# Attention in a decoder trunk: the values product with tokens on the partitions, and scores begun one tile ahead

## The chip, the core and the metric

The kernel runs on one core of a Trainium2 chip. The metric is the device time of one execution in microseconds (us). Runs are compared by their median; the profile is one more execution, read by the hardware profiler.

## What is computed

Two layers of a decoder trunk on 512 tokens of width 1024, float32. Each layer is a feed-forward block, a mixer and a second feed-forward block. The mixer projects the tokens and sends them through three branches: attention with forget gates (FoX), a linear recurrence (RG-LRU) and RWKV-7. The branches are weighted by gates, added and projected. The change is in the attention branch, which has 8 heads of 64:

```
log_f = log_sigmoid(f_logit + f_bias)
F = cumsum(log_f, axis=1)
s = einsum('bhqd,bhkd->bhqk', q, k) * dh**-0.5
s = s + (F[..., :, None] - F[..., None, :])
s = where(kpos <= qpos, s, -inf)
p = softmax(s, axis=-1)
o = einsum('bhqk,bhkd->bhqd', p, v)
```

## The kernel before

Weights are streamed from memory. Large products are made in three passes of float32r halves (`mm3`, lines 201 to 203: hi by hi, lo by hi, hi by lo), so they are nearly all of TensorE's instructions. A weight tile is split into its halves by ScalarE (line 194) and by VectorE or, in the mixer, GpSimd (line 196).

In the mixer, `mix_branches` runs three generators beside each other. FoX attention and then the LRU yield a cost at each step; by the sum of these costs the loop of lines 1140 to 1152 advances the RWKV branch (with raised priority), the gate products (`gates`), and the background work that makes the next modulation (`bg_step`, VectorE line 284). A scheduler then sets a fixed order for each engine from the instructions' order in the program, priorities and its own costs. Each engine works through its list strictly in order; semaphores join the lists.

Attention handles two heads at a time (`fox_pair`, line 1013), so there are four pairs in each layer, eight in all. For a pair it makes q, k and v (lines 1024 to 1040): queries and keys with the 64 channels of a head on the partitions, values with the tokens on the partitions (`vs`). Then come four tiles of 128 queries (line 1047). Tile i sees the n+128 keys up to its own end, n = 128 i, and for each of its two heads:

- GpSimd adds the causal mask to the forget row (`fm`, line 1052);
- TensorE makes the scores, 128 queries on the partitions, in two products (1054, 1055);
- VectorE adds the forget row and finds the maximum, first for the last 128 keys (1058), then for those in front (1062), and negates it (1066);
- ScalarE makes the exponential `e` and its sum (1068);
- VectorE takes the sum's reciprocal (1069) and multiplies `e` by it (1070).

Then, for each head, TensorE transposes the i+1 blocks of `e` (1077) so that keys lie on the partitions, and ScalarE or VectorE copies the result `et` (1080, 1082). The values product (1089) has 64 value columns of one head as its stationary side and 128 queries of `et` moving, and writes head 0 to partitions 0 to 63 and head 1 to 64 to 127 of `po`; ScalarE copies this to `aout` (1091), which has channels on the partitions. Scores, transposes and values products all take PSUM tiles with the tag "s", of which the mixer has three, used in turn (`self.ps("s")`, line 143). `e` has two buffers.

## Time and profile before

| | us |
|---|---|
| median of 3 runs | 3094.02 |
| lowest, highest | 3092.88, 3103.51 |
| the profiled execution | 3098.59 |
| its span | 3096.5 |
| TensorE busy in the span | 2931.2 (95%) |
| VectorE busy | 1880.0 (61%) |
| ScalarE busy | 1142.2 (37%) |
| GpSimd busy | 554.8 (18%) |

PE is TensorE's matmul row, PEld its weight loads, DVE is VectorE, ACT ScalarE, POOL GpSimd, SP the queue that issues most loads. Busy times are of the span. Times in the text are microseconds from the span's start. A matmul's recorded duration includes its way through the array, so neighbours overlap: what one costs is the distance from its start to the next start. A float32 matmul is recorded as two instructions, a transpose as one.

### The profile page before, as it was taken

Reading aid. Unit: us, or ns where it says so; the run is one execution under the profiler, and the core shown is the slowest. Engines: PE = TensorE matmul, PEld = TensorE weight load, DVE = VectorE, ACT = ScalarE, POOL = GpSimd, SP = SyncE. Lnnn points to the kernel's source line nnn. Section 1 sums busy time; section 2 is a strip of 40 time slices with the busy share of each in tenths; the row PEclk is TensorE's granted clock in tenths of the full one; section 3 lists DMA queues with packets and bytes.
Section 4 is the critical chain, followed back from the end, with each engine's and each line's share of the span. In section 5 each row is a group of like instructions: output and inputs, shape, how many; then the busy total and the mean of one; then the engine's idle time right before and its main releaser. Section 6 shows DMA issues by size and latency. Waiting matters only on the chain. (4 is left out here: it accounts for less than half of the span.)

```text
span 3096.5 us, 39351 instructions
## 1 busy us (share of the span) xinstructions
PE 2931.2 (95%) x15330; PEld 2338.4 (76%) x15330; DVE 1880.0 (61%) x3534; ACT 1142.2 (37%) x1699; POOL 554.8 (18%) x379
## 2 busy tenths in 40 slices
PE   7999998998989998999999999889989899999998
PEld 5888886676766788888888887767666677788887
DVE  6755567666785656565656546667676756654435
ACT  4322253332545635222342214433335554342212
POOL 0000142333232013000130002423333320230000
PEclk9999999999999999999999999999999999999999
DMA  8634333333342463434434424433333424632221
GB/s 280 224 109 146 115 117 101 88 87 102 94 113 67 139 203 118 139 122 143 129 117 136 133 92 145 127 99 93 88 90 93 107 73 143 204 116 96 89 68 62
DMA packets 389402, 372.17 MB, mean 120 GB/s; under 512 B 54964, under 2 KB 318544, under 8 KB 389216
## 3 DMA queue, kind: packets, MB, share of 16 engines
q1 hardware_dynamic: 377048, 350.14, 37.0%
q10 hardware_dynamic: 12168, 19.53, 1.7%
q8 instruction: 120, 1.97, 0.3%
q14 instruction: 66, 0.54, 0.1%
HBM read 347.54 MB, written 22.09 MB: 119 GB/s over the span
## 5 line engine op out<-in xcount | busy, mean ns | idle before, releaser
L194 ACT ACTIVATE hi<-raw 128x1024 fp32r<-128x1024 f32 (+1 forms) x460 | 469.2, 1028 | 1248.9 <-PE pg L202 501.3
L196 POOL TENSOR_TENSOR lo<-raw,hi 128x1024 fp32r<-128x1024 f32 x164 | 408.0, 2490 | 1692.1 <-ACT hi L194 1639.2
L201 PE MATMUL pg<-hhi,hi 128*128 128x512 f32 (+1 forms) x1744 | 680.4, 393 | 13.7 <-DVE ks L645 3.7
L202 PE MATMUL pg<-hlo,hi 128*128 128x512 f32 (+1 forms) x1744 | 673.5, 389 | 2.9 <-DVE nm L343 2.9
L203 PE MATMUL pg<-hhi,lo 128*128 128x512 f32 (+1 forms) x1744 | 674.8, 391 | 0.0
L196 DVE TENSOR_TENSOR lo<-raw,hi 128x1024 fp32r<-128x1024 f32 (+1 forms) x296 | 342.5, 1165 | 301.3 <-ACT hi L194 296.1
L201 PEld LDWEIGHTS pg<-hhi,hi 128*128 128x128 f32 x1744 | 330.9, 190 | 86.9 <-issue 10.5
L203 PEld LDWEIGHTS pg<-hhi,lo 128*128 128x128 f32 x1744 | 330.6, 190 | 66.5 <-issue 2.1
L202 PEld LDWEIGHTS pg<-hlo,hi 128*128 128x128 f32 x1744 | 331.2, 190 | 65.3 <-issue 4.7
L202 PE MATMUL pr<-hlo,hi 128*128 128x512 f32 (+1 forms) x816 | 300.4, 368 | 5.1 <-DVE nm L343 2.9
L201 PE MATMUL pr<-hhi,hi 128*128 128x512 f32 (+1 forms) x816 | 301.5, 370 | 2.2 <-ACT hhi L397 2.2
L203 PE MATMUL pr<-hhi,lo 128*128 128x512 f32 (+1 forms) x816 | 300.7, 369 | 0.0
L284 DVE SCALAR_TENSOR_TENSOR acc<-raw,cact,acc 128x512 f32<-128x512 f32 x224 | 187.7, 838 | 48.7 <-DMA raw<-in_ada_w_dram 44.3
L202 PEld LDWEIGHTS pr<-hlo,hi 128*128 128x128 f32 x816 | 155.0, 190 | 34.2 <-issue 7.4
L201 PEld LDWEIGHTS pr<-hhi,hi 128*128 128x128 f32 x816 | 155.1, 190 | 28.1 <-ACT hhi L397 2.6
L203 PEld LDWEIGHTS pr<-hhi,lo 128*128 128x128 f32 x816 | 155.2, 190 | 27.4
L352 POOL TENSOR_TENSOR rstd<-var,mhalf 128x1 f32<-128x1 f32 x48 | 30.2, 630 | 470.5 <-DVE var L351 461.9
L201 PE MATMUL ps<-hi,ahi 128*128 128x512 f32 x264 | 103.5, 392 | 0.0
L203 PE MATMUL ps<-hi,alo 128*128 128x512 f32 x264 | 103.3, 391 | 0.0
L202 PE MATMUL ps<-lo,ahi 128*128 128x512 f32 x264 | 103.1, 391 | 0.0
L480 DVE TENSOR_TENSOR su<-pg,su 128x512 f32<-128x512 f32 x42 | 28.9, 689 | 115.2 <-PE pg L203 115.1
L480 DVE TENSOR_TENSOR su<-pr,su 128x512 f32<-128x512 f32 x42 | 29.0, 690 | 110.0 <-PE pr L203 105.9
(443 smaller groups left out, 4956.9 us busy)
## 6 DMA issues: line engine op xcount, KB each, us to landing
raw<-in_ffn_up_dram SPq DMA_DIRECT2D x70, 1024.0 KB
raw<-in_w_in_dram SPq DMA_DIRECT2D x132, 512.0 KB
raw<-in_ada_w_dram SPq DMA_DIRECT2D x64, 1024.0 KB
raw<-in_ffn_down_dram SPq DMA_DIRECT2D x40, 1024.0 KB
raw<-in_ffn_up_dram SPq DMA_DIRECT2D x36, 512.0 KB
gspill<-gate ACTq DMA_DIRECT2D x48, 256.0 KB
gate<-gspill SPq DMA_DIRECT2D x48, 256.0 KB
ada<-in_ada_w_dram SPq DMA_DIRECT2D x16, 512.0 KB
```

Of the source, the lines that this page charges most:

```text
L194: self.nc.scalar.activation(hi, v, AF.Copy)
L196: eng.tensor_tensor(out=lo, in0=v, in1=hi.bitcast(F32), op=ALU.subtract)
L201: mm(out=ps, lhsT=lhi, rhs=rhi, start=start, stop=False, **kw)
L202: mm(out=ps, lhsT=lhi, rhs=rlo, start=False, stop=False, **kw)
L203: return mm(out=ps, lhsT=llo, rhs=rhi, start=False, stop=stop, **kw).ins
L284: nc.vector.scalar_tensor_tensor(out=acc, in0=r[:, i, :], scalar=c, in1=acc, op0=ALU.mult, op1=ALU.add)
L352: nc.gpsimd.tensor_tensor(out=r, in0=v, in1=self.mhalf, op=ALU.pow)
L480: nc.vector.tensor_tensor(out=su, in0=pss[1], in1=su, op=ALU.mult)
```

## The change

The division is moved behind the values product, the values product is turned round, and the tiles are staggered.

- `scores(i)` holds lines 1048 to 1068 of before. It leaves the exponentials undivided, puts the sums of both heads side by side in one tile `rs` and takes one reciprocal for the two.
- `values(i)` holds the transposes and the values product. `et` is now the stationary side (128 queries wide) and 64 columns of one head's values move; the result has queries on the partitions, head 0 in columns 0 to 63, head 1 in columns 64 to 127. VectorE multiplies it by the reciprocals while it takes it out of PSUM, into `ao`.
- The order in the program is scores 0, scores 1, values 0, scores 2, values 1, scores 3, values 2, values 3. `e` gets four buffers for this.
- After the last tile TensorE transposes the four tiles of `ao`, and ScalarE copies them to `aout` in one instruction of 512 columns where there were four of 128.

```diff
-        for i in range(NT):
+        ao = ap.tile([P, NT, P], F32, tag="ao", bufs=1, name=self.nm("ao"))
+        def scores(i, es, rs):
             n = i * P
-            es = []
             for hh, fb in enumerate(fbs):
...
-                e = ap.tile([P, S], F32, tag="e", bufs=2, name=self.nm("e"))
+                e = ap.tile([P, S], F32, tag="e", bufs=4, name=self.nm("e"))
...
-                rs = self.sp.tile([P, 1], F32, tag="rsum", name=self.nm("rsum"))
-                nc.scalar.activation(e[:, 0 : n + P], e[:, 0 : n + P], AF.Exp, bias=nm, accum_out=rs)
-                nc.vector.reciprocal(rs, rs)
-                nc.vector.tensor_scalar(out=e[:, 0 : n + P], in0=e[:, 0 : n + P], scalar1=rs, scalar2=None, op0=ALU.mult)
+                nc.scalar.activation(e[:, 0 : n + P], e[:, 0 : n + P], AF.Exp, bias=nm, accum_out=rs[:, hh : hh + 1])
                 es.append(e)
                 yield 0.2 * (i + 1)
+            nc.vector.reciprocal(rs, rs)
+
+        def values(i, es, rs):
+            n = i * P
             ets = []
...
             po = self.ps("s")
-            for j in range(i + 1):
-                for hh, et in enumerate(ets):
-                    mm(out=po[64 * hh : 64 * hh + 64, 0:P], lhsT=vs[:, j, hh * 64 : hh * 64 + 64],
-                       rhs=et[:, j * P : (j + 1) * P], start=j == 0, stop=j == i, skip_group_check=True)
-            nc.scalar.activation(self.aout[:, p, n : n + P], po[:, 0:P], AF.Copy)
+            for hh, et in enumerate(ets):
+                for j in range(i + 1):
+                    mm(out=po[:, 64 * hh : 64 * hh + 64], lhsT=et[:, j * P : (j + 1) * P],
+                       rhs=vs[:, j, hh * 64 : hh * 64 + 64], start=j == 0, stop=j == i, skip_group_check=True)
+            nc.vector.tensor_tensor(out=ao[:, i, :].rearrange("p (h d) -> p h d", h=2), in0=po[:, 0:P].rearrange("p (h d) -> p h d", h=2),
+                                    in1=rs.unsqueeze(2).to_broadcast([P, 2, DH]), op=ALU.mult)
             yield 0.25 * (i + 1)
+
+
+        tiles = [([], self.sp.tile([P, 2], F32, tag="rsum", name=self.nm("rsum"))) for _ in range(2)]
+        yield from scores(0, *tiles[0])
+        for i in range(NT):
+            if i + 1 < NT:
+                if i:
+                    tiles.append(([], self.sp.tile([P, 2], F32, tag="rsum", name=self.nm("rsum"))))
+                yield from scores(i + 1, *tiles[i + 1])
+            yield from values(i, *tiles[i])
+        pt = self.ps("s")
+        for i in range(NT):
+            nc.tensor.transpose(pt[:, i * P : (i + 1) * P], ao[:, i, :], self.ident)
+        nc.scalar.activation(self.aout[:, p, :], pt, AF.Copy)
```

In the changed kernel the transposes of `e` have line 1078, the copies of `et` 1081 and 1083, the reciprocal 1070, the values product 1090, the division 1092, and the transposes at the end 1107. The lists of the engines show where the scheduler puts this.

TensorE, the first pair of the first layer, from the scores of tile 0 (lines 1054 and 1055, 128 keys) on; `pg` are other branches' products, `ps` the three tiles in turn. Before:

```order
L1055 MATMUL ps_3940<-kl_3494,q_3575 128x128
L1054 MATMUL ps_3954<-k_3576,q_3575 128x128
L1055 MATMUL ps_3954<-kl_3494,q_3575 128x128
L201 MATMUL pg_4172<-hhi,hi_4173 128x512
...
L1077 MATMUL ps_3966<-ident,e_3943 128x128
...
L1077 MATMUL ps_3970<-ident,e_3957 128x128
L203 MATMUL pg_4172<-hhi,lo_4174 128x512
L1089 MATMUL ps_3974<-et_3968,v_3577 64x128
L1089 MATMUL ps_3974<-et_3972,v_3577 64x128
```

Twelve other products stand between the scores and the first transpose, five between the two transposes, one in front of the values product. Now:

```order
L1055 MATMUL ps_3943<-kl_3494,q_3575 128x128
L1055 MATMUL ps_3954<-kl_3494,q_3575 128x128
L1055 MATMUL ps_3966<-kl_3494,q_3575 128x256
L1055 MATMUL ps_3978<-kl_3494,q_3575 128x256
L201 MATMUL pg_4164<-hhi,hi_4165 128x512
L202 MATMUL pg_4164<-hlo,hi_4165 128x512
L1078 MATMUL ps_4009<-ident,e_3946 128x128
...
L1078 MATMUL ps_4013<-ident,e_3957 128x128
...
L1090 MATMUL ps_4017<-v_3577,et_4011 128x64
L1090 MATMUL ps_4017<-v_3577,et_4015 128x64
```

(Of each score the first product, line 1054, is left out here.) The scores of tile 1 (256 keys) have moved in front of tile 0's transposes, and two other products are left between scores and first transpose, with six between the transposes and six in front of the values product.

VectorE at the same place, from the second head's negated maximum of tile 0 to the copy of `et`; lines 866 and 868 are the RWKV branch, 284 the background work. Before:

```order
L1066 TENSOR_SCALAR nmx_3960<-mx_3958 128x1
L284 SCALAR_TENSOR_TENSOR acc_4204<-raw_4483,cact,acc_4204 128x512
L868 TENSOR_TENSOR Y_3705<-Y_3705,T_3704 64x6x10
L1069 RECIPROCAL rsum_3948<-rsum_3948 128x1
L284 SCALAR_TENSOR_TENSOR acc_4204<-raw_4483,cact,acc_4204 128x512
L866 TENSOR_TENSOR T_3704<-Y_3705 64x63
L1070 TENSOR_SCALAR e_3943<-e_3943,rsum_3948 128x128
...
L1070 TENSOR_SCALAR e_3957<-e_3957,rsum_3962 128x128
L868 TENSOR_TENSOR Y_3705<-Y_3705,T_3704 64x8x8
L1082 COPY et_3968<-ps_3966 128x128
```

Now:

```order
L1066 TENSOR_SCALAR nmx_3960<-mx_3958 128x1
L284 SCALAR_TENSOR_TENSOR acc_4196<-raw_4474,cact,acc_4196 128x512
L868 TENSOR_TENSOR Y_3705<-Y_3705,T_3704 64x6x10
L1058 ISA e_3969,mx_3970<-ps_3966,fm_3964 128x128
L866 TENSOR_TENSOR T_3704<-Y_3705 64x63
L1062 ISA e_3969,mx_3970<-ps_3966,fb_3933,mx_3970 128x128
...
L1070 RECIPROCAL rsum_3939<-rsum_3939 128x2
...
L1062 ISA e_3981,mx_3982<-ps_3978,fb_3935,mx_3982 128x128
L866 TENSOR_TENSOR T_3704<-Y_3705 64x63
L1066 TENSOR_SCALAR nmx_3985<-mx_3982 128x1
L1083 COPY et_4011<-ps_4009 128x128
```

The divisions of `e` are gone, and the reading of tile 1's scores has come in between, in front of the copy of tile 0's `et`.

TensorE at the end of the same pair. Now:

```order
L1090 MATMUL ps_4203<-v_3577,et_4140 128x64 x3
L1078 MATMUL ps_4218<-ident,e_4122 128x128 x4
L1090 MATMUL ps_4242<-v_3577,et_4216 128x64 x4
L1107 MATMUL ps_4252<-ident,ao_3938 128x128 x2
L1090 MATMUL ps_4242<-v_3577,et_4223 128x64 x4
L1107 MATMUL ps_4252<-ident,ao_3938 128x128
L201 MATMUL pg_4261<-hhi,hi_4265 128x512
L202 MATMUL pg_4261<-hlo,hi_4265 128x512
L1107 MATMUL ps_4252<-ident,ao_3938 128x128
```

The four new transposes (1107) stand among the last values products; between the last of these and the last transpose, which needs its division, are one transpose and two other products.

## Rows read from the trace of the kernel before

**Rows 1.** The page: the span, and busy time by engine.

```profile
span 3096.5 us, 39351 instructions
PE 2931.2 (95%) x15330; PEld 2338.4 (76%) x15330; DVE 1880.0 (61%) x3534; ACT 1142.2 (37%) x1699; POOL 554.8 (18%) x379
```

**Rows 2.** Groups of TensorE: count, busy us, mean ns, idle before, releaser.

```profile
L1089 PE MATMUL ps<-et,v 128*64 128x128 f32 x320 | 37.8, 294 | 2.0 <-DVE T L866 2.0
L1077 PE MATMUL ps<-ident,e 128*128 128x128 f32 x160 | 30.7, 284 | 25.7 <-DVE e L1070 25.4
```

**Rows 3.** Sum over windows around the eight pairs: busy us by engine.

```profile
sum 346.00, PE 310.81 PEld 229.07 DVE 258.86 ACT 129.78 POOL 107.37; mean PE 38.85 PEld 28.63 DVE 32.36 ACT 16.22 POOL 13.42
```

**Rows 4.** Timeline of TensorE, first pair: start, duration, instruction, idle before.

```profile
502.40 0.28 PE L1055 MATMUL ps<-kl,q 128*128 128x128 f32 x1
...
504.87 0.39 PE L202 MATMUL pg<-hlo,hi 128*128 128x512 f32 x1
505.10 0.40 PE L203 MATMUL pg<-hhi,lo 128*128 128x512 f32 x1
508.25 0.33 PE L1077 MATMUL ps<-ident,e 128*128 128x128 f32 x1 [2.75 <-DVE e L1070]
...
518.96 0.41 PE L1077 MATMUL ps<-ident,e 128*128 128x128 f32 x2 [1.83 <-DVE e L1070]
...
533.79 0.66 PE L1077 MATMUL ps<-ident,e 128*128 128x128 f32 x4 [1.66 <-DVE e L1070]
```

**Rows 5.** Timeline of the other engines during the first of these waits.

```profile
503.28 2.41 POOL L196 TENSOR_TENSOR lo<-raw,hi 128x1024 fp32r<-128x1024 f32 x1 [5.47 <-ACT hi L194]
...
503.49 2.28 DVE L866 TENSOR_TENSOR T<-Y 64x60 f32<-64x60 f32 x1
503.58 0.39 ACT L1068 ACTIVATE e<-e,nmx 128x128 f32<-128x128 f32 x1
...
505.69 0.14 DVE L1066 TENSOR_SCALAR nmx<-mx 128x1 f32<-128x1 f32 x1
...
507.92 0.27 DVE L1070 TENSOR_SCALAR e<-e,rsum 128x128 f32<-128x128 f32 x1
```

**Rows 6.** Groups of VectorE.

```profile
L1070 DVE TENSOR_SCALAR e<-e,rsum 128x128 f32<-128x128 f32 (+3 forms) x64 | 39.9, 624 | 0.9
L1058 DVE CUSTOM_DVE_ANT_0 e<-ps,fm 128x128 f32<-128x128 f32 x64 | 18.5, 289 | 41.2 <-PE ps L1055 40.1 <-issue 0.7
```

**Rows 7.** Windows: stretch, length, TensorE busy (count), mean granted clock, DMA share, GB/s.

```profile
508.00:514.00 6.00, 5.75 (x23) 0.72 0.85 226
744.00:752.00 8.00, 7.20 (x22) 0.57 0.00 0
770.00:776.00 6.00, 6.00 (x27) 0.72 0.69 194
2040.00:2046.00 6.00, 5.72 (x23) 0.72 0.87 229
```

**Rows 8.** Timeline of TensorE: the values product, and what starts after it.

```profile
519.30 0.43 PE L1089 MATMUL ps<-et,v 128*64 128x128 f32 x2
519.66 0.44 PE L1054 MATMUL ps<-k,q 128*128 128x384 f32 x1
...
536.10 1.09 PE L1089 MATMUL ps<-et,v 128*64 128x128 f32 x14
537.11 0.50 PE L202 MATMUL pg<-hlo,hi 128*128 128x512 f32 x1
```

**Rows 9.** Timeline of TensorE: products with 128 weight columns and few moving ones.

```profile
464.30 0.95 PE L747 MATMUL pr<-heads,sq 128*128 128x2 f32 x8
465.11 0.48 PE L202 MATMUL pg<-hlo,hi 128*128 128x512 f32 x1
...
546.24 0.55 PE L913 MATMUL pc<-S,AR 128*128 128x64 f32 x4
546.73 0.45 PE L916 MATMUL pc<-UV,AM 128*64 128x64 f32 x4
```

More of the change, by code (lines that the diff above doesn't have):

```diff
@@ L989, in fox_prelude @@
                                      start=k0 == 0 and h is self.hhi, stop=k0 == 4 and h is self.hlo, skip_group_check=True)
-        yf = ap.tile([P, S], F32, tag="e", bufs=2, name=self.nm("yf"))
+        yf = ap.tile([P, S], F32, tag="e", bufs=4, name=self.nm("yf"))
         nc.vector.tensor_copy(yf, ps)
@@ L1004, in fox_prelude @@
             nc.tensor.transpose(ps[0:H, t * P : (t + 1) * P], sp[:, t, :], self.ident)
-        nF = ap.tile([P, S], F32, tag="e", bufs=2, name=self.nm("nF"))[0:H, :]
+        nF = ap.tile([P, S], F32, tag="e", bufs=4, name=self.nm("nF"))[0:H, :]
         ones = self.ones[0:H, :].to_broadcast([H, S])
@@ L1034, in fox_pair @@
         yield 5.2
-        vf = ap.tile([P, S], F32, tag="e", bufs=2, name=self.nm("vf"))
+        vf = ap.tile([P, S], F32, tag="e", bufs=4, name=self.nm("vf"))
         nc.vector.tensor_copy(vf, self.gemm("av", p))
```

## The prediction

> **What bounds the kernel now.** I read the page first: TensorE is busy for 2931 of 3096.5 us, VectorE for 1880 [rows 1]. TensorE is the bound nearly everywhere, so the kernel gets faster only where TensorE stands still, runs at the lower clock, or is given less to do. Then the groups of TensorE's instructions: the transposes of the exponentials (line 1077) stood idle for 25.7 us in front of them, 25.4 of it until VectorE had divided e (line 1070), and the values products (1089) for 2.0 [rows 2]. That is 27.7 us in all, 0.9% of the span, and nothing else that the change touches can give more.
>
> Then the stretches in which the eight head pairs (four in each of two layers) work on their scores. All eight together last 346 us, TensorE is busy for 311 of them and VectorE for 259 [rows 3]. So VectorE is three quarters full where TensorE waits for it, and a wait is not only the length of the chain but the queue in front of it.
>
> The timeline of the first pair shows one such wait from both sides. TensorE does the scores of both heads of tile 0 until 502.5, has other products until 505.5, one in 0.23 us, and begins the transpose at 508.25 after 2.75 us of nothing [rows 4]. On VectorE, line 866 of the RWKV branch, with 60 elements in a partition, takes 2.28 us, from 503.49 until GpSimd's subtraction (line 196, 503.28 to 505.69) is over. Behind it stand the second head's negated maximum at 505.69, and line 1070 of the first head, which comes at 507.92 although its exponential was done at 504.0 [rows 5]. The division itself took only 0.27 us: the wait is the queue, and each step of the chain that is on VectorE has to stand in it once more.
>
> **The change, part by part.** *The chain.* Before: scores, maximum, negation, exponential, reciprocal, division, transpose. Now the transpose needs the exponential alone, and the scores of tile i+1 stand ahead of tile i's transposes. If this hid everything it would give back 27.7 us [rows 2]; if the queue only moved, nothing. I walked the first pair through the new order with durations from rows. The first transpose could start at about 504.05, after the exponential [rows 5], against TensorE's arrival at about 503.6 (the scores of two tiles and two products): a wait of 0.4 us. The second one uses the PSUM slot of the next tile's first scores (the pool has three, taken in turn), so VectorE must have read these: after 505.69 five instructions stand in front of that (lines 284, 868, 1058, 866, 1062), as many and of like size as stood in front of line 1070 before, which took 2.2 us [rows 5]. So it starts at about 507.9, and TensorE is there at 505.6, six products after the first: a wait of 2.3. The values product then waits some 0.5 (an estimate) for the copied et, which stands behind the next tile's second head on VectorE. That is 3.2 us at tile 0, where 2.75 stood; tiles 1 to 3, begun ahead, I put at 0.8 together, where 1.83 and 1.66 stood [rows 4]: 4.0 us in place of 6.2. Pairs in which VectorE is less locked should do better. I take half of 27.7: **-13 us**.
>
> *The clock.* Behind four of these waits the granted clock falls to its lower level (1.2 GHz in place of 2.4). The stretches have mean granted clocks of 0.72, 0.57, 0.72 and 0.72 over 6, 8, 6 and 6 us [rows 7]; 6x0.28+8x0.43+6x0.28+6x0.28 = 8.5 us lost. If all waits went, 8.5 would come back; I take half: **-4 us**.
>
> *VectorE.* It loses 64 divisions (39.9 us) and half of the short reciprocals, and gets 32 divisions of a 128x128 product read from PSUM; the nearest row is line 1058, 128x128 from PSUM, at 289 ns: 9.3 us [rows 6]. It is relieved of 31 us and the reciprocals. Most of that is already in the waits above; for other work in these stretches that TensorE awaits from VectorE I take **-2 us** (bounds 0 and -5).
>
> *The values product.* Each of the 160 products runs as two recorded instructions. Before, two heads go to two halves of the array's columns, 64 weight columns each, and 128 columns stream. A run of 2 takes 0.36 us and one of 14 1.01 [rows 8], so (1.01-0.36)/12 = 0.054 each and 0.25 to start and end a run; the order has 33 runs in each layer: 320x0.054+66x0.25 = 34 us. Now 128 weight columns are loaded for 64 that stream. The same shape stands at line 913: a run of 4 takes 0.49; line 747, as many weights with 2 columns streaming, takes 0.81 for 8 [rows 9]. So the weights set it, 0.101 each, and 0.08 for a run. With 38 runs a layer by the order: 320x0.101+76x0.08 = 38 us. If a run costs 0.25 as before, 51. So between +4 and +18; I take **+5**, since line 913 is the same shape between the same neighbours.
>
> The Trainium skill ("TensorEngine Tiling (Array Packing)", Performance Considerations) speaks against this edit: where the moving side is 64 or shorter it advises to swap the operands, so that the short side is stationary and two column tiles work side by side, for up to twice the speed; the old code has that form and the new one gives it up. By it alone 17 us of streaming would become 35. The rows agree on the single instruction (0.054 against 0.101), but not on whole runs, where the packed form pays 0.25 to begin.
>
> *The transposes at the end.* Four new ones in each pair, 32 in all; line 1077 took 30.7 us for 160 [rows 2], 0.19 each: **+6 us**. The 32 copies on ScalarE become 8; ScalarE is not waited for there, so nothing. The last of the four waits for VectorE's division of the last tile with two products as its only cover; that wait is inside the half that I kept.
>
> *Moved past queues.* GpSimd's masks (1052) of the next tile now stand behind the same weight subtraction; they are in the walk. DMA issues on SP shift by a few places among weight loads, hidden by buffers that are loaded ahead.
>
> Sum: -13-4-2+5+6 = -8 us. The profiled execution took 3098.6, the median of the runs is 3094.0, so I put it against the median: **3086 us**, or -0.26%. What a measurement can tell from no change is 0.5%, 15.5 us.
>
> **Rivals.**
> A (forecast, 0.40): half of the wait goes. 3086, between 3074 and 3100.
> B (0.20): the queue was the division's own fault, since line 1070, with a mean of 624 ns [rows 6] where one of 128 columns took 0.27 [rows 5], was itself held up; without it all waits go: -27.7-8.5-2+11 = -27, 3067. For it: 25.4 us are booked on that line alone. Against it: in the first wait the delay sat in line 866, which stays.
> C (0.17): the wait only changes its name, from the division to the reading of PSUM and the copy of et, or the scheduler takes the lead away again (in the fourth pair it puts sixteen other products between the scores of tile 0 and the last of tile 1's): no gain, +11: 3105. For it: VectorE is as full as before, in a shorter stretch.
> D (0.10, slower): the three PSUM slots. If the second transpose of every tile with one begun ahead (24 of them) waits for VectorE to read the next scores, as I found for tile 0 (2.3 us), that is 55 in place of 27.7, and with the work 55-28+11 = +38: 3132. It decides where the VectorE work ahead of that reading exceeds the cover on TensorE, some six products or 1.4 us. Against it: later tiles have more cover and less of the RWKV lines between.
> E (0.13): the values product costs its upper bound, +18: 3099. Against it: line 913. The rule of the Trainium skill (TensorEngine Tiling (Array Packing), Performance Considerations) would come out here too.
>
> **How the numbers follow.** Faster by over 0.5% (under 3078.5): nearly all of B (0.17) and the lower edge of A (0.10): 0.27. Slower (over 3109.5): D and the upper edge of C: 0.14. Within: 0.59. The range of 3064 to 3108 holds A, E, most of B and C, and leaves out D and the tails. Its ends are also the bounds of the terms: all waits and clock gained (-30), against none gained and the work at +11 to +15.
>
> **What would show it.** Right: idle time in front of the transposes 10 to 16 us, its releaser no longer a division; some of it in front of the values product or the new transposes at the end; the values product 36 to 42 us busy; VectorE's busy time over 31 us less; the clock's dips after the first pair shorter but not gone. Wrong: idle time under 5 us (B), or as large as before behind lines that read PSUM (C, D); over 45 us for the values product (E). A change outside the eight stretches of more than 5 us would mean that the shifted order of the other branches decides, which I priced at nothing.

## The result, and the profile after

The changed kernel takes 3128.51 us (median of 4 runs, 3126.61 to 3133.75) where the kernel before took 3094.6 in the same comparison: a ratio of 1.0106, 95% interval 1.0083 to 1.013. It is slower by 34 us; the forecast was 8 us faster, and the range ended at 3108. The profiled execution has a span of 3132.0 us, beside 3096.5 [rows 1].

The page after, its span and busy times:

```profile
span 3132.0 us, 39339 instructions
PE 2952.7 (94%) x15362; PEld 2363.6 (75%) x15362; DVE 1871.5 (60%) x3470; ACT 1137.0 (36%) x1675; POOL 552.6 (18%) x379
```

VectorE has 64 instructions fewer and is relieved of only 8.5 us, where 31 were forecast. TensorE is busy for 21.5 us more.

Groups of TensorE after, in attention (count, busy us, mean ns, idle before, releaser):

```profile
L1090 PE MATMUL ps<-v,et 128*128 128x64 f32 x320 | 48.8, 279 | 8.4 <-DVE et L1083 8.0
L1078 PE MATMUL ps<-ident,e 128*128 128x128 f32 x160 | 32.6, 281 | 8.2 <-DVE mx L1062 6.0 <-ACT e L1067 1.8 <-DVE nmx L1066 0.2
L1054 PE MATMUL ps<-k,q 128*128 128x128 f32 (+3 forms) x64 | 22.8, 366 | 9.9 <-DVE mx L1058 9.9
L1107 PE MATMUL ps<-ident,ao 128*128 128x128 f32 x32 | 8.8, 330 | 0.0
```

No wait for a division is left. In its place stand waits for VectorE's copy of et, for its reading of earlier scores, whose PSUM slot is wanted, and 1.8 us for the exponential: 8.4+8.2+9.9 = 26.5 us, where 27.7 stood [rows 2].

So attention is not where 34 us went. The next view is the windows over the two mixers, from the RWKV branch's first wait at line 822 to the merge (stretch, length, busy by engine, granted clock, DMA share, GB/s). Before:

```profile
477.30:1038.30 561.00, 510.91 (x3059) 382.22 (x3058) 379.62 (x920) 243.25 (x414) 167.37 (x111) 0.97 0.33 91
2008.90:2571.00 562.10, 513.26 (x3059) 383.79 (x3058) 379.31 (x920) 243.30 (x414) 166.76 (x111) 0.97 0.33 91
```

After:

```profile
477.50:1050.20 572.70, 519.53 (x3075) 394.45 (x3074) 373.55 (x889) 240.51 (x402) 166.72 (x112) 0.96 0.33 89
2020.60:2606.30 585.70, 526.61 (x3074) 399.79 (x3074) 376.69 (x888) 240.66 (x402) 165.42 (x111) 0.95 0.32 87
```

The mixers grew from 1123.1 to 1158.4 us; all the rest of the span stayed at 1973.5. I split the 35.3 us by adding up, from the timeline, the idle time in front of each TensorE instruction, and, from windows of 2 us, length times (1 - granted clock); attention's part is from a pair's first scores to its last product, and a dip of the clock that begins there counts with it:

| both mixers, us | before | after | difference |
|---|---|---|---|
| idle in attention's stretches | 31.9 | 29.7 | -2.2 |
| idle elsewhere in the mixers | 66.4 | 81.2 | +14.8 |
| lost to the granted clock (of it in attention's stretches) | 32.3 (10.2) | 47.8 (15.4) | +15.5 (+5.2) |
| the rest: work | 992.4 | 999.7 | +7.3 |

The work came out near its price (11 us), and attention's waits moved without shrinking much. 25 us, 14.8 of idle time and 10.3 of clock, lie in the other branches, which the change does not touch. The waits of TensorE by line, in total (us, times, longest) show where. Before:

```profile
PE ps L1039 <- DVE vf L1036: 8.0, 4, 3.2
PE pr L844 <- DVE T L881: 5.4, 4, 2.2
PE pr L756 <- DVE rw L753: 5.1, 4, 2.4
```

After:

```profile
PE pr L756 <- DVE rw L753: 11.8, 7, 3.1
PE pg L201 <- DVE rst L333: 9.6, 2, 4.8
PE pr L844 <- DVE T L881: 7.8, 4, 4.1
PE pg L201 <- DVE kl L1032: 4.8, 2, 2.4
PE ps L1039 <- DVE vf L1036: 2.2, 4, 0.8
```

The wait at line 333 is new and, at 4.8 us, the longest in the mixers. It stands in the RWKV branch's rsqrt, far from attention, once in each layer. The timeline of VectorE, GpSimd and TensorE there, first layer (start, duration, instruction, idle before):

```profile
856.13 2.40 POOL L196 TENSOR_TENSOR lo<-raw,hi 128x1024 fp32r<-128x1024 f32 x1
856.23 2.85 DVE L957 TENSOR_TENSOR Yt<-Yt,gsum 128x512 f32<-128x512 f32 x1
...
861.07 2.37 POOL L196 TENSOR_TENSOR lo<-raw,hi 128x1024 fp32r<-128x1024 f32 x1 [2.55 <-ACT hi L194]
861.12 2.36 DVE L330 TENSOR_SCALAR rsq<-rst 128x8 int32<-128x8 int32 x1
...
864.38 0.75 DVE L1251 SCALAR_TENSOR_TENSOR xc<-pg,vcol,xc 128x511 f32<-128x511 f32 x1
...
866.85 0.76 PE L201 MATMUL pg<-hhi,hi 128*128 128x512 f32 x1 [4.79 <-DVE rst L333]
```

Two instructions of VectorE take 2.85 and 2.36 us, each until just after a subtraction of GpSimd beside it has ended; line 330 has 8 elements in a partition. Behind them in VectorE's list stand the three readings of `pg` by the LRU's convolution (line 1251), and TensorE wants that PSUM slot. (The view names line 333 because it ends within 0.1 us of the third of these readings.) In the kernel before, the same readings (line 1235 there) stood earlier in VectorE's list, between lines 954 and 961, no subtraction ran beside line 957, and nothing waited. In the new wait a later place in the list and two subtractions come together. The clock follows the wait (windows, as above):

```profile
860.00:864.00 4.00, 2.05 (x9) 1.34 (x8) 3.83 (x9) 1.66 (x3) 2.37 (x1) 1.00 0.46 124
864.00:868.00 4.00, 1.15 (x3) 0.99 (x4) 3.80 (x12) 1.18 (x2) 0.00 (x0) 0.57 0.51 131
868.00:872.00 4.00, 4.00 (x12) 2.62 (x11) 1.30 (x2) 0.08 (x1) 0.00 (x0) 0.57 0.00 0
```

TensorE stood still from 862 to 866.8, and the granted clock fell to its lower level (1.2 GHz) up to about 872: 8x0.43 = 3.4 us more. By this reckoning the one place, in two layers, costs 2x(4.8+3.4) = 16 us; what it was worth in a run comes below.

### The profile page after: what moved, and what is told of

It reads as the page before. It is cut to its first block, busy times and chain, and to the rows that moved or that the text cites. A ratio compares the mean times of both kernels' runs of the same rounds, so it can differ in the third digit from the quotient of the medians.

```text
span 3132.0 us, 39339 instructions
## 1 busy us (share of the span) xinstructions
PE 2952.7 (94%) x15362; PEld 2363.6 (75%) x15362; DVE 1871.5 (60%) x3470; ACT 1137.0 (36%) x1675; POOL 552.6 (18%) x379
## 5 line engine op out<-in xcount | busy, mean ns | idle before, releaser
L202 PE MATMUL pg<-hlo,hi 128*128 128x512 f32 (+1 forms) x1744 | 680.4, 393 | 2.9 <-DVE nm L343 2.9
L202 PEld LDWEIGHTS pg<-hlo,hi 128*128 128x128 f32 x1744 | 332.6, 191 | 66.4 <-issue 5.2
L284 DVE SCALAR_TENSOR_TENSOR acc<-raw,cact,acc 128x512 f32<-128x512 f32 x224 | 177.7, 793 | 42.6 <-DMA raw<-in_ada_w_dram 38.1
```

Source lines behind the costliest of these rows:

```text
L202: mm(out=ps, lhsT=lhi, rhs=rlo, start=False, stop=False, **kw)
L284: nc.vector.scalar_tensor_tensor(out=acc, in0=r[:, i, :], scalar=c, in1=acc, op0=ALU.mult, op1=ALU.add)
```

## The experiments

There were three theories at the start. **Theory 1**: the lead makes new waits, through the three PSUM slots (rival D). **Theory 2**: the scheduler dealt the lists of all engines in the mixer anew, and VectorE's instructions of other branches meet GpSimd's subtractions at worse places; later split into 2a, an accident of this order, and 2b, a consequence of the change's shape. **Theory 3**: the turned product and its transposes cost more than priced. All ratios are to the kernel before on the same chip (3091 to 3094 us).

**Parts of the change alone.** No lead: scores and values of a tile follow each other.

```diff
...
+        for i in range(NT):
...
+            yield from scores(i, *tile)
+            yield from values(i, *tile)
```

> The changed kernel with the lead taken back: scores of tile i, then values of tile i; the values product stays turned and the division behind it. Theory 1 (the lead's waits: with three PSUM slots, scores and transposes of a tile wait until VectorE has read the next tile's scores): most of the loss of 34 us goes, 3092 to 3105, and the waits of the scores' and transposes' products on VectorE's reads of PSUM (some 16 us now) fall under 6. Theory 2 (the list of every engine in the mixer came out another way, and VectorE's work of the other branches now meets GpSimd's subtractions at worse places): the time is anywhere between 3080 and 3130, and idle outside the eight score stretches does not follow the lead. Theory 3 (the turned product and its transposes cost more than was recorded): no change, 3120 or more.

Measured: 3118.95, ratio 1.0081 (1.0064 to 1.0097).

The lead alone: the kernel before, divisions and old values product kept, cut into `scores` and `values` with scores one tile ahead and four buffers of `e`.

```diff
...
+        yield from scores(0, tiles[0])
+        for i in range(NT):
+            if i + 1 < NT:
+                yield from scores(i + 1, tiles[i + 1])
+            yield from values(i, tiles[i])
```

> The kernel before with the lead alone: scores of the next tile are begun ahead, e has four buffers; the division of e, the values product and the copies are as before. Theory 1: slower than before by 15 to 35 us, as the waits come with the lead. Theory 2: anywhere between -15 and +35. Theory 3: no loss, within 10 us of before.

Measured: 3113.07, ratio 1.0062 (1.0043 to 1.0081).

The change with fewer PSUM slots used: in tiles 0 and 1 both heads share one tile of "s" for their scores, and one for their transposes.

```diff
-                sc = self.ps("s")
...
+                if hh == 0:
+                    bank = self.ps("s")
+                sc = bank[:, 256 * hh : 256 * hh + 256]
```

> The changed kernel, in which the scores of both heads of tiles 0 and 1 share one PSUM tile, and their transposes too, so that these tiles take half as many of the three slots. Theory 1: the waits of line 1054 on line 1058 (9.9 us) and of tile 0's transposes on line 1062 go, 10 to 25 us faster than the changed kernel, 3103 to 3118. Theory 2: these waits go as well, but the time moves by something else, in either direction.

Measured: 3113.74, ratio 1.0065 (1.0048 to 1.0082). Idle time in attention fell to 18.0 us (26.5 in the changed kernel).

No part carries the whole loss. Without the lead, TensorE's waits for VectorE's reading of scores are gone (15.9 us in the changed kernel), others stand in their place (11.0 us for the exponential, 9.0 for et), and three quarters of the loss stay: against theory 1 as the main cause. Without the turned product 0.62% stay: against theory 3. The times of the second and third runs also lie within what theory 1 had given, so they alone don't decide; but in the third the wait on line 1058 that was to go (9.9 us) is still 8.3. All three, like the changed kernel, have the same two 4.8 us waits at line 333 and the same 4.8 us in all at line 1032.

**The order moved and nothing else.** The pace constant decides how fast the other branches advance beside attention. First the kernel before:

```diff
-FOX_COST, LRU_COST = 24.5, 11.9
+FOX_COST, LRU_COST = 25.0, 11.9
```

> The kernel before with one number of the pacing changed (FOX_COST 25.0 in place of 24.5), which leaves every computation as it is and shifts the other branches' steps a little against attention; the engines' lists change in about as many rows as by the change itself. Theory 1: within 6 us of before. Theory 2: off by 10 us or more, in either direction, with idle and clock losses at other places.

Measured: 3098.89, ratio 1.0026 (1.0015 to 1.0036): 7.5 us, between what the two theories gave. Then the changed kernel, at 25.0 and at 24.0:

> The changed kernel with one number moved: the pace constant for an attention pair is 25.0 in place of 24.5, so the other branches are advanced a little more slowly beside attention; no product, copy or buffer differs. The kernel before, moved in the same way, came out at 1.0026 of itself. Theory 2a (the loss of 34 us outside the score stretches is an accident of the lists: which VectorE work meets which GpSimd subtraction): the accident is dealt anew, so the time moves by 8 us or more against the changed kernel, to either side; I expect 3105 to 3122, a ratio of 1.004 to 1.010, and the 4.8 us wait for the RWKV branch's rsqrt in each layer gone or changed. Theory 2b (the shape of the change costs it: attention's own stretches got shorter by 5 us each, so more of the other branches' products stand without attention's work between them): the time stays within 5 us of 3126, ratio 1.0095 to 1.0125, and the 4.8 us waits stay. Theory 3 (dearer products) also gives 3126.

Measured: 3100.60, ratio 1.0029 (1.0018 to 1.004), a little under what 2a gave, and far from 2b and 3. The 4.8 us waits at line 333 are gone.

> The changed kernel with the pace constant for an attention pair at 24.0 in place of 24.5: the other branches are advanced a little faster. Theory 2a (accident of the lists): the time moves by 8 us or more, to either side, anywhere in 3100 to 3140, and the two variants of the pace differ from each other. Theory 2b (the shape of the change) and theory 3 (dearer products): within 5 us of 3126, ratio 1.0095 to 1.0125.

Measured: 3103.98, ratio 1.0037 (1.0025 to 1.0049). That the two paces would differ from each other, as 2a had it, is not shown (3.4 us, and the intervals overlap). But two thirds of the 1.06% go when one number of the order moves by 2%, in either direction. Theory 2b falls, and theory 3 with it as the main cause.

**GpSimd's subtractions taken away.** In the mixers VectorE makes the low halves of the weights (line 196), in the kernel before and in the changed one:

```diff
...
-        self.wide, self.on_pool = False, True
+        self.wide, self.on_pool = False, False
...
```

> The kernel before, but in the mixer VectorE and not GpSimd makes the subtractions that split the weights (line 196). No VectorE instruction can then be held up while such a subtraction runs; VectorE has more to do, some 107 us in the eight stretches alone. It is the base for the next run. I expect it slower than the kernel before, 3110 to 3180, since VectorE was three quarters full in these stretches; if the stretching of VectorE's instructions beside the subtractions was most of the wait, it could come out level, 3090 to 3100.

> The changed kernel with the same edit: VectorE splits the weights in the mixer. To be read against the run before it (the kernel before with this edit). Theory 2a in the form that VectorE's instructions meet GpSimd's subtractions at worse places: with no such subtraction the difference of the two shrinks from 34 us to within -10 to +12 us, and VectorE's busy time falls by the divisions in full (30 us or more less than in the run before it, where the changed kernel showed only 8.5 less than before). Theory 2b (the shape) and theory 3 (dearer products, which are worth 7 us by the accounting): the difference stays at 25 us or more under 2b, 5 to 12 under theory 3 alone.

Measured: 2990.51, ratio 0.9669 (0.9654 to 0.9683), and 2975.58, ratio 0.9623 (0.9607 to 0.9639). My expectation for the first was wrong by sign: it is 101 us faster. And the change, 34 us slower with GpSimd's subtractions, is now 15 us faster, beyond the bound I had set. Page of the kernel before with this edit:

```profile
span 2989.8 us, 39327 instructions
PE 2894.8 (97%) x15330; PEld 2319.4 (78%) x15330; DVE 1884.8 (63%) x3662; ACT 1138.2 (38%) x1699; POOL 250.5 (8%) x251
```

VectorE makes 128 more subtractions of 1.22 us, 157 us of work, and is busy for 1884.8 us where it was 1880.0 [rows 1]: some 150 us of its busy time before had been standing still. The traces give nearly the same when each VectorE instruction is set against the shortest record of the same form (operation, tiles, shape) in any run here: those that overlap in time with a weight subtraction on GpSimd take 173 us too long in the kernel before, and 24 with this edit, beside the subtractions that GpSimd still makes behind the mixers. In the changed kernel it is 174: the change did not add to the standing still, it moved it. Groups of the two kernels show what the change does then. Before, with this edit:

```profile
L1089 PE MATMUL ps<-et,v 128*64 128x128 f32 x320 | 36.1, 287 | 0.0
L1070 DVE TENSOR_SCALAR e<-e,rsum 128x128 f32<-128x128 f32 (+3 forms) x64 | 24.6, 389 | 0.6
```

The changed kernel with this edit, its page and groups:

```profile
span 2972.5 us, 39303 instructions
PE 2892.5 (97%) x15362; PEld 2335.8 (79%) x15362; DVE 1867.8 (63%) x3598; ACT 1135.8 (38%) x1675; POOL 254.1 (9%) x251
...
L1090 PE MATMUL ps<-v,et 128*128 128x64 f32 x320 | 42.7, 268 | 0.2
L1107 PE MATMUL ps<-ident,ao 128*128 128x128 f32 x32 | 6.7, 277 | 0.0
L1092 DVE TENSOR_TENSOR ao<-ps,rsum 128x128 f32<-128x128 f32 x32 | 9.2, 286 | 9.9 <-PE ps L1090 9.5
```

The divisions removed had cost 24.6 us, not the 39.9 of [rows 6], and VectorE falls by 17. By the same accounting as above, the mixers go from 1019.5 to 1000.2 us: idle -14.8, clock -6.8, work +2.4. (The two profiled executions differ by 17.3 us, the medians by 15.)

**Is it the standing still, or that VectorE is quicker with the low halves?** The changed kernel with VectorE's split, and GpSimd makes each of the mixers' 128 subtractions once more for nobody:

```diff
         eng.tensor_tensor(out=lo, in0=v, in1=hi.bitcast(F32), op=ALU.subtract)
...
+            self.nc.gpsimd.tensor_tensor(out=g, in0=v, in1=hi.bitcast(F32), op=ALU.subtract)
```

> The changed kernel with VectorE splitting the weights in the mixer (2975.6 us, 0.9623 of the kernel before), and beside it GpSimd makes each of these 128 subtractions once more, into a tile that nobody reads. No instruction on the path waits for GpSimd's result; the weight buffers are held until it has read them, as in the kernel before. Theory 2a (VectorE's instructions are held up while such a subtraction runs, and this is what the 100 us are): most of it is lost again, 3040 to 3110, ratio 0.983 to 1.006, VectorE's busy time rises by 100 us or more without an instruction more. Rival (the gain came because VectorE makes the low halves in 1.2 us where GpSimd takes 2.4, so that products start earlier): the time stays within 10 us of 2976, VectorE's busy time within 15 us.

Measured: 3193.81, ratio 1.0326 (1.0311 to 1.0341), 218 us over the same kernel without the extra subtractions and beyond the bound of 2a. Its page:

```profile
span 3193.7 us, 39587 instructions
PE 2967.5 (93%) x15362; PEld 2381.5 (75%) x15362; DVE 2051.5 (64%) x3598; ACT 1136.6 (36%) x1675; POOL 609.9 (19%) x379
```

VectorE's same 3598 instructions are busy for 184 us more. The rival (quicker low halves) falls, and the waits say it without this run: in the kernel before no wait of TensorE ended with a low half of a weight (line 196), and here two did, 1.1 us in all. Another rival, that GpSimd's other work no longer queues behind the subtractions, falls by the same view: VectorE's waits for results of GpSimd are 39.7 us in the kernel before and 42.5 with VectorE's split.

**The parts again, with VectorE's split**, lead alone and no lead, edits as above:

> The old values product and the old division in front of the transposes, scores one tile ahead with four buffers for e, and VectorE splitting the weights in the mixer. Against the kernel before with that split (2990.5) the whole change gave -14.9 us. By the waits in front of the transposes (3.4 us) and the four buffers alone the lead can give 3 to 6; if the lead carries the gain, 2976 to 2981; if the moved division does, 2986 to 2992.

> The turned values product with the division behind it and the four transposes at the end, tiles one after the other, and VectorE splitting the weights in the mixer. Against the kernel before with that split (2990.5): theory 3 (the turned product and its transposes cost more than they give) 2990 to 3000; the prediction's own terms (+5 and +6 for TensorE, -2 for VectorE, half of the lost waits) 2990 to 2998; if relieving VectorE of the divisions carries the gain, 2976 to 2984.

Measured: 2979.21, ratio 0.9633 (0.9619 to 0.9647), and 2987.18, ratio 0.9659 (0.9644 to 0.9673), beside 0.9669 for the kernel before with the split and 0.9623 for the whole change. The second lies between the cases of its expectation. By the medians, three quarters of the gain come with the lead; that the moved division and turned product alone gain a quarter, or nothing, lies within the intervals.

**No subtraction of weights on GpSimd at all**; the 36 behind the mixers go to VectorE too:

```diff
-                self.on_pool = c == 0 and not begin
+                self.on_pool = False
```

> The changed kernel with no weight subtraction on GpSimd anywhere: the 36 that it still made behind the mixers (93.9 us of GpSimd) go to VectorE too. If VectorE's instructions are held up beside them there as well, and TensorE feels it there: 2955 to 2972, ratio 0.956 to 0.961. If that stretch has room on VectorE: within 4 us of 2975.6, ratio 0.961 to 0.9636.

Measured: 2969.07, ratio 0.9603 (0.9587 to 0.9619), the fastest of all: 4% under the kernel before, 5% under the changed one. The last step, from 0.9623, is within the intervals.

**Does the order matter only through GpSimd?** The paces once more, with VectorE's split:

> The kernel before with VectorE splitting the weights in the mixer and the pace constant for an attention pair at 25.0 in place of 24.5. With the split on GpSimd this move of the pace was worth +7 us. If the lists matter through VectorE's instructions beside GpSimd's subtractions: within 5 us of 2990.5, ratio 0.965 to 0.9687. If the lists matter by themselves: it may move by 8 us or more.

> The changed kernel with VectorE splitting the weights in the mixer and the pace constant at 25.0. With the split on GpSimd this move of the pace was worth -26 us. If the lists matter through VectorE's instructions beside GpSimd's subtractions: within 5 us of 2975.6, ratio 0.9605 to 0.964, and 10 to 20 us below the run before it. If the lists matter by themselves: it may move by 8 us or more, and the gain of the change (15 us) may go with it.

> The changed kernel with VectorE splitting the weights in the mixer and the pace constant at 24.0. With the split on GpSimd this move was worth -23 us. If the lists matter through VectorE's instructions beside GpSimd's subtractions: within 5 us of 2975.6, ratio 0.9605 to 0.964. If the lists matter by themselves: 8 us or more away from it, to either side.

Measured: 2991.66 (0.9674, 0.966 to 0.9689), 2982.48 (0.9649, 0.9633 to 0.9665), 2996.30 (0.9691, 0.9677 to 0.9706). The first is as expected. The second, 7 us above 2975.6 and 9 below the first, lies between its cases. The last is not as expected: at pace 24.0 the changed kernel loses 21 us without any subtraction on GpSimd in the mixers. In its waits of TensorE stands now the reading of `pg` by the LRU:

```profile
PE pg L201 <- DVE xc L1251: 8.7, 7, 1.9
```

So an order can be bad by itself.

**Two subtractions of 64.** In each mixer of the changed kernel only the 47th and 48th go to VectorE, those beside lines 957 and 330 in the timeline above:

```diff
...
+        self.count += self.on_pool
+        eng = self.nc.gpsimd if self.on_pool and self.count not in (47, 48) else self.nc.vector
```

> The changed kernel with 2 of the 64 weight subtractions of each mixer, the 47th and 48th, made by VectorE instead of GpSimd; the other 62 stay. These are the two that run beside VectorE's lines 957 (2.85 us) and 330 (2.36 us), behind which TensorE waits 4.8 us in each layer for the rsqrt of the RWKV branch. VectorE's list keeps its order there. If these two instructions are held up by the subtractions beside them: they take 0.7 and 0.2 us, the wait falls from 4.8 to under 1.5 us in each layer, and with the granted clock that fell behind it (3.4 us in each layer) the time falls by 8 to 16 us, 3110 to 3118, ratio 1.005 to 1.008. If the order of VectorE's list makes the wait: VectorE has 1.2 us more ahead of it twice, the wait stays at 4 us or more and the time within 4 us of 3126.

Measured: 3111.09, ratio 1.0054 (1.0037 to 1.0071). VectorE's timeline at the same place (lines are 2 higher: 959 was 957, 332 was 330), and TensorE's:

```profile
860.43 0.69 DVE L959 TENSOR_TENSOR Yt<-Yt,gsum 128x512 f32<-128x512 f32 x1
861.04 1.22 DVE L198 TENSOR_TENSOR lo<-raw,hi 128x1024 fp32r<-128x1024 f32 x1
863.51 0.17 DVE L332 TENSOR_SCALAR rsq<-rst 128x8 int32<-128x8 int32 x1
863.66 1.22 DVE L198 TENSOR_TENSOR lo<-raw,hi 128x1024 fp32r<-128x1024 f32 x1
...
867.45 0.47 PE L203 MATMUL pg<-hhi,hi 128*128 128x512 f32 x1 [0.52 <-DVE rst L335]
```

The two instructions take 0.69 and 0.17 us, the wait is 0.52 in place of 4.79, the granted clock stays at 1.00, and the ratio falls from 1.0106 to 1.0054, some 16 us. Not all of that is won here. Set beside the changed kernel's trace instruction by instruction, TensorE gains 6.4 us at this place in the first layer and 6.7 in the second: 13 us of the 34. The lists are also not quite the same: three steps of the rsqrt (0.6 us) now come behind the first reading of `pg` and not ahead of it, and TensorE has three more products (0.7 us) to do in front of the wait. So for some 10 to 13 us of the loss the subtractions are the cause, shown at its place. The rest of what the two profiled executions differ by comes and goes elsewhere: with the same order around it, the wait of line 1054 in the first pair of a layer is 0.6 us in layer 1 and 3.6 in layer 2 in the changed kernel, and 3.6 and 0.3 in this run. There VectorE reached its line 284 some 0.8 us later against the scores in layer 2 (after a DMA) than in layer 1, and so met a subtraction (2.92 us in place of 0.75): which instruction is held up can turn on less than a microsecond.

**The third point of the kernel before**, pace 24.0, with GpSimd's and with VectorE's split:

> The kernel before with the pace constant at 24.0, the third point beside 24.5 (3092) and 25.0 (3099). If the change as such costs time beside GpSimd's subtractions: 3085 to 3100, below the 3104 of the changed kernel at this pace. If this pace is a worse order for both, 3104 to 3125.

> The kernel before with VectorE splitting the weights in the mixer and the pace constant at 24.0, the third point beside 24.5 (2990.5) and 25.0 (2991.7). If the 20 us that the changed kernel lost at this pace (2996) belong to the pace: 3000 to 3012, and the change gains at all three paces. If they belong to the changed kernel's lists: 2988 to 2995.

Measured: 3143.38, ratio 1.0161 (1.0146 to 1.0176), which neither case of the expectation held, and 3001.98, ratio 0.9707 (0.9691 to 0.9724), as the first case gave: without the subtractions the 20 us belong to the pace. The first has its waits of TensorE where the changed kernel has them at 24.5, and worse:

```profile
PE pg L201 <- DVE xc L1235: 14.3, 7, 4.1
PE pg L201 <- DVE kl L1032: 13.6, 4, 4.5
```

All twelve points, as ratios to the kernel before:

| pace | before | changed | change | VectorE splits: before | changed | change |
|---|---|---|---|---|---|---|
| 24.0 | 1.0161 | 1.0037 | -1.24% | 0.9707 | 0.9691 | -0.16% |
| 24.5 | 1 | 1.0106 | +1.06% | 0.9669 | 0.9623 | -0.46% |
| 25.0 | 1.0026 | 1.0029 | +0.03% | 0.9674 | 0.9649 | -0.25% |

With GpSimd's subtractions the order is worth 1.6% in the kernel before and 0.8% in the changed one, more than the change; the mean over the three paces is -0.05%. Without them the order is worth 0.4 and 0.7%, and the change gains at each pace, by 0.29% in the mean (the intervals of the two kernels overlap at 24.0 and, slightly, at 25.0).

## Why the prediction was wrong

**The step that failed** is the last of the parts: GpSimd's masks and SP's loads were walked through, and the order of the other branches was priced at nothing. The prediction named the sign of it (a change of more than 5 us outside the eight stretches); it was 25 us, and 10 to 13 of them are shown at one place in the rsqrt of another branch. Of the 43 us between the forecast (-8) and the two profiled executions (+35), 27 lie in this step, counting the 2 that VectorE was to give outside the chain; 20 lie in attention's waits and clock, and the work gave 4 back. The loop over the branches advances RWKV, gates and background by attention's steps, so with these in a new order VectorE's list changed far from attention too, and against 64 subtractions of GpSimd in each mixer another order is another deal, that is, another chance of what meets what. What I took as the measure of the kernel before, 3094, was itself a lucky deal: 3143 and 3099 were its neighbours.

*The chain, -13.* Measured -1.2 (27.7 to 26.5). The walk of the first pair was right in kind and near in size, if not in its places: 4.0 us forecast, 4.3 measured (1.8 for the exponential, 0.6 and 1.9 for the reading of PSUM), where 6.2 stood. Carrying it to all pairs as one half, more than the walk itself gave, was the optimism (and half of 27.7 is 13.9, not 13): I had seen line 866 held up beside a subtraction [rows 5] and kept that queue, but no reason stood behind the half. Without the subtractions the same instructions wait 1.4 us in all (0.2 at line 1090, 0.5 at 1078, 0.7 at 1054), so the queue was GpSimd's doing, as rows 5 had shown without my drawing the conclusion.

*The clock, -4.* Measured +5.2 in attention's stretches, +15.5 in both mixers: it followed the waits, and these grew elsewhere.

*VectorE.* 31 us were to be relieved, 8.5 were: 39.9 us for the divisions [rows 6] held 15 us of standing still (24.6 without the subtractions). Rival B had seen that much, that line 1070 was itself held up; but the standing still as a whole stayed (173 us, now 174), and other instructions took it over, as line 957 did: 5.5 us for its 8 before, now

```profile
L957 DVE TENSOR_TENSOR Yt<-Yt,gsum 128x512 f32<-128x512 f32 x8 | 14.2, 1780 | 0.1
```

*The values product, +5, and the transposes, +6.* These were right in sign and too high: 7.3 us of work were measured, 11 forecast. The group reads 48.8 us, above the bound of 45 that I had set for E, but a recorded duration grows at the lower clock (line 201: 0.39 us at granted 1.00, 0.63 at 0.57). From start to next start the products take 33.0 us before and 35.7 now, +2.7, and the transposes 3.4; without the subtractions 30.7 and 32.5, +1.8, and 2.7. That is under the lower bound of +4. The 38 us that I added up come out again with other terms: by the two runs of rows 9 a product costs 0.08 and a run 0.17, not 0.101 and 0.08.

The Trainium skill (TensorEngine Tiling (Array Packing), Theoretical Speedup) gives up to twice the speed for a dimension of 64 that is packed. The trace agrees on long runs and not on short ones: at full granted clock a run of 16 instructions took 1.02 us in the packed form and takes 1.73 now, a run of 2 took 0.36 and takes 0.19. In all, giving up the packed form cost 6% without the subtractions (30.7 to 32.5 us).

*The rivals.* D had nearly the right time, 3132, for a reason that carries 15.9 us (9.9+6.0 in front of lines 1054 and 1078) where it asked for 55. C came nearest in kind, the wait only changed its name, but its price of 3105 held no loss outside. The sum, -0.26%, comes near what the change is worth in the mean where GpSimd stays quiet in the mixers (-0.29%). That is chance: there the transposes had only 3.4 us of waits to give, not 27.7 (line 1077 on line 1070), so the terms of the sum do not carry over.

*Open.* The rest of the loss was not taken apart by runs. The trace of the changed kernel goes a step further: in VectorE's list an instruction held up beside a subtraction stands shortly ahead of both waits on line 1032 and of all four long waits on line 753, as here in the first layer:

```profile
712.94 2.90 DVE L957 TENSOR_TENSOR Yt<-Yt,gsum 128x512 f32<-128x512 f32 x1
718.64 0.69 DVE L1032 TENSOR_TENSOR kl<-pg,k 64x512 fp32r<-64x512 f32 x1
...
887.11 2.23 DVE L335 SCALAR_TENSOR_TENSOR rsq<-rst,rsq 128x8 f32<-128x8 f32 x1
889.38 0.43 DVE L753 COPY rw<-rsq 128x512 f32<-128x512 f32 x1
```

The waits on line 881 are another matter: in the longest, 4.1 us, VectorE itself had been idle until a DMA landed. That the loss moves with the order is shown; what each of these waits would be worth without its subtraction is not. Why pace 24.0 is a bad order even without the subtractions was not tried.

## What to carry to other kernels

Where a scheduler deals the lists from costs, one order against one order measures the deal as well: move a pace constant in both kernels first, and do not credit a change with less than that spread (here 1.6 and 0.8%). Before costing a removed instruction by its row, look at what runs beside it on GpSimd: the shortest duration of the same form was its own cost here, and the rest passed to other instructions. And ask of every helper that an idle GpSimd took over what it does to VectorE's short instructions: here giving the work back to VectorE left its busy time nearly as it was (1880.0 to 1884.8 us) and took 3.3% off the kernel.

## What the runs showed of the hardware

While GpSimd subtracts one 128x1024 tile from another (2.4 us), some instructions of VectorE stand still until it ends, even one with 8 elements in a partition, and others don't notice. In the changed kernel (count, shortest, median and longest ns, first and last start):

```profile
L957 DVE TENSOR_TENSOR Yt<-Yt,gsum x8: 685/1770/2899, 575.8 to 2563.4; 128x512 f32<-128x512 f32 x8
L330 DVE TENSOR_SCALAR rsq<-rst x16: 163/172/2357, 465.9 to 2565.9; 128x8 int32<-128x8 int32 x16
```

A sum along a row of a tile in SBUF is not held up. In the changed kernel none runs beside a subtraction, but in the kernel before one does (line 954), and keeps its 0.69 us:

```profile
853.85 2.39 POOL L196 TENSOR_TENSOR lo<-raw,hi 128x1024 fp32r<-128x1024 f32 x1 [2.40 <-ACT hi L194]
855.16 0.69 DVE L954 TENSOR_REDUCE gsum<-Yt 128x8 f32<-128x512 f32 x1
```

Line 957 (two tiles from SBUF) and line 330 (one tile with constants) are held up. Lines that read PSUM are not: of line 1251's readings of `pg` 19 run beside a subtraction, none of them over 0.75 us, and line 1058 has a mean of 289 ns in the kernel before [rows 6] and 287 with VectorE's split. The Trainium skill (SBUF — State Buffer, "SBUF: two separate sides") says this: VectorE and GpSimd share one pair of ports, which the one that starts first locks for its whole instruction, against VectorE's instructions with two inputs from SBUF or in a two-port mode. The trace agrees in which are held up and for how long (0.17 to 2.36 us, 0.69 to 2.85). What it cost I had not expected: taking the mixers' subtractions off GpSimd was worth 101 us of 3092, and adding them for nobody cost 218. TensorE's clock went with it: the mean granted clock over the span is 0.969 with the added subtractions, 0.983 before, 0.979 changed, and 0.996 with no weight subtraction on GpSimd.
